# An encoder layer with split weights: high and low activations pass a rounded weight together in one 512-column matmul, and key products on 64 rows

## The chip, the core and the metric

The kernel runs on one core of a Trainium2 chip. Five engines work side by side: TensorE (matmuls; PE in the profile, its weight loads PEld), VectorE (DVE), ScalarE (ACT), GpSimd (POOL) and SyncE (SP, which here only issues transfers). TensorE writes its results into PSUM banks of 128 x 512 float32; VectorE and ScalarE read them there. Transfers run on 16 shared DMA engines. The metric is the device time of one execution, in microseconds, as the median of several runs.

## The reference

One layer of an encoder over 256 tokens of 2048 features, everything in float32:

```python
def reference(x, mem, ...):
    h = layer_norm(x, ln_in_g, ln_in_b)
    for l in range(DEPTH):                      # DEPTH = 1
        mix = hybrid_mixer(h, w_in[l], ...)
        h = layer_norm(ALPHA * h + mix, ln1_g[l], ln1_b[l])
        xa = memory_cross_attention(h, mem, ...)
        h = layer_norm(ALPHA * h + xa, ln2_g[l], ln2_b[l])
        ff = swiglu(h, ffn_wg[l], ffn_wu[l], ffn_wd[l])
        h = layer_norm(ALPHA * h + ff, ln3_g[l], ln3_b[l])
    return h
```

The mixer multiplies h by one wide matrix w_in and feeds two recurrences over time from its columns: a gated linear one (RG-LRU, with a convolution over four steps before it) and a matrix-valued one with 32 heads of 64 (RWKV-7), in which each step rewrites a 64 x 64 state: `S = S*w - (S kk) b^T + v k^T`, output `S r`. Both are gated, added and multiplied by w_out. Then follow attention with 4 heads over 256 memory tokens, and the feed-forward part `(silu(h wg) * (h wu)) wd` with 5632 inner features.

## The kernel before

**Products with streamed weights.** Every large matrix is read once, in halves of 128 x 1024 float32 (512 KB). Matmuls run in a reduced float32 type. To keep precision, each operand is split into two parts: the value rounded to that type (high) and the remainder (low). `split_half` (lines 146 to 156) loads a half into one of four buffers, ScalarE makes the high part `wh` (line 153), VectorE the low part `wl` (line 155), into three buffers each. Of the four products high x high, high x low, low x high and low x low the last is left out.

`wstat` (lines 158 to 169) is used where the result is wanted with features on partitions: a tile of 128 output features by 256 tokens, summed over 16 blocks of 128 input features, eight blocks in each half. The weight block is stationary (loaded into the array), the activations move. For each block line 164 multiplies `wh` by the high activations and line 165 the same `wh` by the low ones, 256 columns each; after eight blocks line 168 multiplies the eight `wl` blocks by the high activations. So a half has 24 matmuls of 256 columns, and a tile uses half a bank. `wtile` (line 174) takes a bank and calls it; its result is a region of PSUM that the consumer reads. It is called for the early and late memory keys (312, 812), all columns of w_in (361, 498, 674, 688, 695, 727), queries (827) and the gate and up products (886, 889). `xstat` (line 179) is the other form, for w_out, the memory values, the attention's output and the down product: there the activations are stationary and 512 columns of the weights move (lines 192, 193, 196). High and low activations are separate tiles of 128 x 256 that `pair_tiles` (line 204) makes.

**The mixer.** For each of four groups of heads (`rwkv_group`), each with four tiles, `tile_stage` (line 425) asks for the tiles k, r and v of w_in and defers the small work on them by a number of weight halves: `key_direction` normalises the key, builds the products' left operand `bk` and copies it on POOL's queue into the padded tile `bz` (lines 458 and 459), in which each head of 64 rows has its own copy with zeros in the other 64 rows; `receptance` fills the other half of the right operand `kr` (465, 466); `products` (line 487) multiplies, for each of two heads and four chunks of 64 steps, 128 padded rows of `bz` by `kr`, in one bank per head, and line 493 masks each bank into `gt`. When a group is complete, `recurrence` solves a triangular system by 31 pairs of small VectorE instructions (lines 532 to 537), sends the result through memory, and after a wait counted in weight halves (`PACE`) `chunk_steps` runs the recurrence over chunks (line 557 on). Between these stand the tiles of the other recurrence (`lru_pair`, line 655, with `recurrent_gates` at 658) and the gates (`gate_group`, line 724).

**What sets the order.** A planner orders each engine's instructions at compile time: it follows priorities (`stream` puts weight loads, splits and the reading of finished banks ahead of all else) and modelled times. At run time each engine keeps that order and waits at its head. Two instructions that touch the same bank are kept apart. In the mixer two accumulator banks serve `wtile`, later four. The pool `mixps` (tag `mix`) has two banks for the small products.

Of the kernel before, what the change touches and what calls it, by code (L numbers as in the profile page):

```python
# [18 lines left out]
P = 128  # L19
T = 256  # L20
# [26 lines left out]
def trunk(ctx, tc, x, memT, vec, rows, consts, lruw, loraw, w_in, w_out, wq, wk, wv, wo, wgu, wd, out,  # L47
# [50 lines left out]
    accs = [None]  # L98
    dram = ctx.enter_context(tc.tile_pool(name="dram", bufs=1, space=bass.MemoryType.DRAM))

    # ---------------------------------------------------------------- constants
# [43 lines left out]
    # ---------------------------------------------------------------- streamed products  # L145
# [11 lines left out]

    def wstat(src, xh, xl, acc):
        for hf in range(2):
            h, l = split_half(src, hf)  # L160
            for kk in range(8):
                k = hf * 8 + kk
                w = h[:, kk * P:(kk + 1) * P]
                nc.tensor.matmul(acc, w, xh[k], start=(k == 0), stop=False)  # L164
                nc.tensor.matmul(acc, w, xl[k], start=False, stop=False)  # L165
            for kk in range(8):
                k = hf * 8 + kk
                mm = nc.tensor.matmul(acc, l[:, kk * P:(kk + 1) * P], xh[k], start=False, stop=(k == 15))  # L168
# [5 lines left out]
    def wtile(src, xh, xl):  # L174
        a = new_acc()[:, 0:T]
        wstat(src, xh, xl, a)
        return a
# [25 lines left out]

    def pair_tiles(pool, n, tag):
        hs = [pool.tile([P, T], F32R, name=f"{tag}h{k}", tag=f"{tag}h{k}") for k in range(n)]
        ls = [pool.tile([P, T], F32R, name=f"{tag}l{k}", tag=f"{tag}l{k}") for k in range(n)]
        return hs, ls

    # ---------------------------------------------------------------- layer norm
# [51 lines left out]
    # ================================================================ input norm  # L261
    h0_d = dram.tile([P, 2, 2048], F32, name="h0_d")
    xTh, xTl = pair_tiles(base, NK, "xT")
    # ================================================================ mixer
# [4 lines left out]
    with ExitStack() as mx:  # L269
# [14 lines left out]
        # ---- first memory keys while the input is normalised  # L284
# [26 lines left out]
        def early_key(k):  # L311
            a = wtile(wk[k], mTh, mTl)
            kr = boot.tile([P, T], F32, name="kr", bufs=2)
            with stream(32):
                nc.scalar.copy(kr, a)
# [21 lines left out]
        # ---- persistent buffers with zeroed parts  # L337
        bz = grp.tile([P, 2, 4, P], F32, name="bkz")
        nc.gpsimd.memset(bz, 0.0)
# [18 lines left out]
        # ---- low-rank inputs  # L358
# [11 lines left out]
        def decay_rates(g, jp, rates):  # L370
            # ---- decay and in-context rate, two tiles
# [53 lines left out]
        def tile_stage(g, j, i, u, fs, av, ev, dt, kr, bkt, sv, yb, gt):  # L425
# [3 lines left out]
            def key_direction():  # L429
                # even chunk: [r'|kk'], [k''|b']; odd chunk: [kk'|r'], [b'|k'']  # L430
# [592 lines left out]
```

## Time and profile before

| | |
|---|---|
| three runs, median | 2201.14 us |
| lowest and highest run | 2199.56 and 2203.24 us |
| the profiled execution, span | 2197.7 us |
| mean granted TensorE clock | 0.990 |
| weight data read and other reads, whole run | 375 MB at a mean of 175 GB/s with the writes |

The profiled execution's own time is its span, from the first instruction to the last; no other time is given for it. By stage, from the view of windows (busy microseconds in each):

| stage | from and to, us | PE | DVE | ACT |
|---|---|---|---|---|
| keys, input norm, mixer | 0 to 970 | 931 | 720 | 512 |
| w_out, attention | 970 to 1440 | 456 | 293 | 212 |
| gate and up products | 1440 to 1940 | 500 | 253 | 216 |
| down product | 1940 to 2183 | 240 | 117 | 92 |
| last norm, output | 2183 to 2198 | 0 | 11 | 2 |

How to read the profile's lines: a group's line has the line of the kernel, the engine, the operation, what it writes and reads (by the program's names), shapes and count; then the total busy time in microseconds, the mean of one in nanoseconds, and the idle time of the engine just before such instructions, with what ended most of it. A timeline line has start, duration, engine, line, operation and, in brackets, the idle time before. A TensorE matmul's duration covers its way through the array and overlaps with that of its neighbours. A float32 matmul of the mixer's small products (not of the reduced type) leaves two records. A window's line has its length, busy time and count for PE, PEld, DVE, ACT and POOL, then the granted TensorE clock, the share of DMA engines at work and GB/s.

### The profile page before, as it was taken

To read this page: it belongs to the slowest core of one execution; us is meant where nothing else is said; L and a number is where in the kernel's file an instruction comes from. 1 tells how busy PE (TensorE), PEld (TensorE's weight loads), DVE (VectorE), ACT (ScalarE), POOL (GpSimd) and SP (SyncE) were. 2 spreads that over 40 slices of the span, in tenths; PEclk is the share of its full clock that TensorE was granted. 3 is DMA by queue.
4 is the path that set the end of the run, shared out by engine and by line. 5 is a ranking of instruction groups with operands and counts; after the bars stand their busy time and mean duration, and the time that the engine had idled before them with its cause. 6 is when DMAs were issued, how large, how long until landed. Compare 5 with 4: busy or idle time off the path is not lost.

```text
span 2197.7 us, 38943 instructions
## 1 busy us (share of the span) xinstructions
PE 2127.7 (97%) x15952; PEld 2004.9 (91%) x15952; DVE 1394.3 (63%) x2121; ACT 1031.9 (47%) x1442; POOL 102.8 (5%) x137
## 2 busy tenths in 40 slices
PE   7999999999999999989999999999999999999996
PEld 7999899999999999877988998799999999988885
DVE  7778676967695769567854555674444444444445
ACT  6646444554455445554544444354444444443332
POOL 1200010011001100200100000000000000000001
PEclk9999999999999999999999999999999999999998
DMA  8555445554555465467565545566555555555563
GB/s 301 186 166 172 140 130 171 177 153 139 176 168 154 139 180 183 123 223 247 183 206 194 165 140 165 190 198 200 184 182 183 184 184 183 182 188 194 192 193 124
DMA packets 149939, 392.41 MB, mean 179 GB/s; under 512 B 39296, under 2 KB 58624, under 8 KB 149248
## 3 DMA queue, kind: packets, MB, share of 16 engines
q1 hardware_dynamic: 137776, 368.81, 52.6%
q10 hardware_dynamic: 9296, 13.24, 2.4%
q0 software_dynamic: 2688, 7.87, 1.2%
q8 instruction: 125, 2.05, 0.4%
q14 instruction: 54, 0.44, 0.1%
HBM read 375.05 MB, written 10.62 MB: 175 GB/s over the span
## 4 chain that ended last, share of the span: by engine, by line
PE 82%; DVE 8%; DMA 6%; issue 2%; ACT 2%; ACTq 0%; POOL 0%; SPq 0%; DVEq 0%; POOLq 0%
PE acc L168 17%; PE acc L165 17%; PE acc L164 17%; PE acc L193 7%; PE acc L192 7%; PE acc L196 7%; DVE wl L155 3%; DVE pd L534 2%; DMA gb<-in_rows_dram 1%; PE mix L491 1%; DVE xi L537 1%; PE rec L590 1%; PE rec L615 1%; DMA bkz<-bk 1%; PE rec L597 1%
## 5 line engine op out<-in xcount | busy, mean ns | idle before, releaser
L155 DVE TENSOR_TENSOR wl<-raw,wh 128x1024 fp32r<-128x1024 f32 x656 | 800.7, 1222 | 581.9 <-ACT wh L153 539.7
L153 ACT CAST wh<-raw 128x1024 fp32r<-128x1024 f32 x656 | 687.4, 1049 | 869.6 <-PE acc L165 535.2
L164 PE MATMUL acc<-xTh,wh 128*128 128x256 f32 x3520 | 881.1, 287 | 1.5 <-DVE ge L694 0.8
L165 PE MATMUL acc<-xTl,wh 128*128 128x256 f32 x3520 | 875.7, 285 | 1.2 <-DVE xTl L248 0.8
L165 PEld LDWEIGHTS acc<-xTl,wh 128*128 128x128 f32 x3520 | 677.9, 193 | 4.5 <-DVE xTl L248 1.2
L164 PEld LDWEIGHTS acc<-xTh,wh 128*128 128x128 f32 x3520 | 677.3, 193 | 4.8 <-DVE ge L694 1.4
L168 PE MATMUL acc<-xTh,wl 128*128 128x256 f32 x3520 | 503.8, 284 | 1.3 <-DVE wl L155 1.3
L168 PEld LDWEIGHTS acc<-xTh,wl 128*128 128x128 f32 x3520 | 457.0, 192 | 3.6 <-DVE wl L155 2.1
L193 PE MATMUL acc<-wh,fl 128*128 128x512 f32 x352 | 136.9, 389 | 0.0
L192 PE MATMUL acc<-wh,fh 128*128 128x512 f32 x352 | 136.9, 389 | 0.0
L196 PE MATMUL acc<-wl,fh 128*128 128x512 f32 x352 | 108.4, 389 | 0.0
L196 PEld LDWEIGHTS acc<-wl,fh 128*128 128x128 f32 x352 | 66.1, 188 | 13.8
L193 PEld LDWEIGHTS acc<-wh,fl 128*128 128x128 f32 x352 | 66.1, 188 | 13.7
L192 PEld LDWEIGHTS acc<-wh,fh 128*128 128x128 f32 x352 | 66.0, 188 | 13.6
L534 DVE TENSOR_TENSOR pd<-xi,al 128x2 f32<-128x2 f32 (+30 forms) x124 | 63.0, 508 | 2.4
L603 POOL TENSOR_SCALAR dms<-ct,dm 128x128 f32<-128x128 f32 x48 | 39.1, 826 | 496.4 <-DVE smat L609 423.3
L890 DVE TENSOR_TENSOR fsg<-fsg,acc 128x256 f32<-128x256 f32 x44 | 18.5, 420 | 61.9 <-PE acc L168 61.4
L192 PE MATMUL acc<-wh,Ah 128*128 128x512 f32 x128 | 50.6, 395 | 0.0
L193 PE MATMUL acc<-wh,Al 128*128 128x512 f32 x128 | 50.6, 395 | 0.0
L192 PE MATMUL acc<-wh,oTh 128*128 128x512 f32 x128 | 49.9, 390 | 0.0
L193 PE MATMUL acc<-wh,oTl 128*128 128x512 f32 x128 | 49.8, 389 | 0.0
L193 PE MATMUL acc<-wh,Bl 128*128 128x512 f32 x128 | 49.8, 389 | 0.0
(267 smaller groups left out, 2265.4 us busy)
## 6 DMA issues: line engine op xcount, KB each, us to landing
raw<-in_w_in_dram SPq DMA_DIRECT2D x232, 512.0 KB, 4.0
raw<-in_wgu_dram SPq DMA_DIRECT2D x176, 512.0 KB, 4.7
raw<-in_wd_dram SPq DMA_DIRECT2D x88, 512.0 KB, 4.6
raw<-in_wk_dram SPq DMA_DIRECT2D x32, 512.0 KB, 4.8
raw<-in_w_out_dram SPq DMA_DIRECT2D x32, 512.0 KB, 5.3
raw<-in_wv_dram SPq DMA_DIRECT2D x32, 512.0 KB, 4.8
raw<-in_wq_dram SPq DMA_DIRECT2D x32, 512.0 KB, 4.1
raw<-in_wo_dram SPq DMA_DIRECT2D x32, 512.0 KB, 4.4
```

The lines of the kernel that those rows point to most:

```text
L153: nc.scalar.copy(h, raw)
L155: nc.vector.tensor_tensor(l, raw, h.bitcast(F32), ALU.subtract)
L164: nc.tensor.matmul(acc, w, xh[k], start=(k == 0), stop=False)
L165: nc.tensor.matmul(acc, w, xl[k], start=False, stop=False)
L168: mm = nc.tensor.matmul(acc, l[:, kk * P:(kk + 1) * P], xh[k], start=False, stop=(k == 15))
L192: nc.tensor.matmul(pt[tt], xh[k][:, ts], w, start=(first and kk == 0), stop=False)
L193: nc.tensor.matmul(pt[tt], xl[k][:, ts], w, start=False, stop=False)
L196: nc.tensor.matmul(pt[tt], xh[k][:, ts], l[:, kk * 512:(kk + 1) * 512], start=False, stop=(last and kk == 1))
L491: nc.tensor.matmul(ps[:, c * P:(c + 1) * P], bz[:, hh, c, :], kr[:, c, :], start=True, stop=True)
L534: nc.vector.tensor_tensor(pd[:, 0:nj, 0:t + 1], xi[:, 0:nj, 0:t + 1], al[:, 0:t + 1, t].rearrange("p (o s) -> p o s", o=1) .broadcast_to([ ...
L537: nc.vector.tensor_reduce(xi[:, 0:nj, t], pd[:, 0:nj, 0:t + 1], AX.X, ALU.add, negate=True)
L603: nc.gpsimd.tensor_scalar(dms[:, j * P:(j + 1) * P], smask, dm[:, j, c:c + 1], None, ALU.mult)
```

## The change

High and low activations of a block become the two halves of one tile of 128 x 512 (`pair`), and lines 164 and 165 become one matmul of 512 columns whose result fills a whole bank: the left half sums high x high, the right half high x low. Line 168 adds low x high to the left half as before. When a tile's sum is complete, `wtile` has ScalarE copy the right half to SBUF and VectorE add the left half to it, in a pool `joins` with two buffers for each; its result is now an SBUF tile, and all consumers read that. Where the old code copied a finished bank to SBUF at once (early keys, line 315; the convolution's input, line 677), the add writes there and the copy is gone. In the key products the padded tile `bz`, its zeroing and its two copies per tile are gone: each product takes the 64 rows of its head from `bk` and `kr` directly, and the two heads alternate, chunk by chunk, between two banks that are taken together.

```diff
+    joins = [None]
+    joins[0] = ctx.enter_context(tc.tile_pool(name="joins", bufs=2))
...
+    both, keep = {}, []
+
     def wstat(src, xh, xl, acc):
         for hf in range(2):
             h, l = split_half(src, hf)
             for kk in range(8):
                 k = hf * 8 + kk
                 w = h[:, kk * P:(kk + 1) * P]
-                nc.tensor.matmul(acc, w, xh[k], start=(k == 0), stop=False)
-                nc.tensor.matmul(acc, w, xl[k], start=False, stop=False)
+                nc.tensor.matmul(acc, w, both[id(xh[k])], start=(k == 0), stop=False)
             for kk in range(8):
                 k = hf * 8 + kk
-                mm = nc.tensor.matmul(acc, l[:, kk * P:(kk + 1) * P], xh[k], start=False, stop=(k == 15))
+                mm = nc.tensor.matmul(acc[:, 0:T], l[:, kk * P:(kk + 1) * P], xh[k], start=False,
+                                      stop=(k == 15))
             passed(mm.ins)
...
-    def wtile(src, xh, xl):
-        a = new_acc()[:, 0:T]
+    def wtile(src, xh, xl, out=None):
+        a = new_acc()
         wstat(src, xh, xl, a)
-        return a
+        with stream(32):
+            t = joins[0].tile([P, T], F32, name="jl")
+            nc.scalar.copy(t, a[:, T:2 * T])
+            if out is None:
+                out = joins[0].tile([P, T], F32, name="js")
+            nc.vector.tensor_tensor(out, a[:, 0:T], t, ALU.add)
+        return out
...
+    def pair(pool, name, tag):
+        t = pool.tile([P, 2 * T], F32R, name=name, tag=tag)
+        h = t[:, 0:T]
+        both[id(h)] = t
+        keep.append(h)
+        return h, t[:, T:2 * T]
+
     def pair_tiles(pool, n, tag):
-        hs = [pool.tile([P, T], F32R, name=f"{tag}h{k}", tag=f"{tag}h{k}") for k in range(n)]
-        ls = [pool.tile([P, T], F32R, name=f"{tag}l{k}", tag=f"{tag}l{k}") for k in range(n)]
-        return hs, ls
+        ps = [pair(pool, f"{tag}{k}", f"{tag}{k}") for k in range(n)]
+        return [h for h, _ in ps], [l for _, l in ps]
...
         def early_key(k):
-            a = wtile(wk[k], mTh, mTl)
             kr = boot.tile([P, T], F32, name="kr", bufs=2)
-            with stream(32):
-                nc.scalar.copy(kr, a)
+            wtile(wk[k], mTh, mTl, out=kr)
             nc.sync.dma_start(k_d[k], kr)
...
-        bz = grp.tile([P, 2, 4, P], F32, name="bkz")
-        nc.gpsimd.memset(bz, 0.0)
...
-                nc.gpsimd.dma_start(bz[0:64, 0], bk[0:64])
-                nc.gpsimd.dma_start(bz[64:128, 1], bk[64:128])
                 q["bk"], q["kf"] = bk, kf
...
             def products():
+                pt = [mps(), mps()]
+                for c in range(4):
+                    for hh in range(2):
+                        rows = slice(64 * hh, 64 * hh + 64)
+                        nc.tensor.matmul(pt[hh][:, c * P:(c + 1) * P], q["bk"][rows, c, :], kr[rows, c, :],
+                                         start=True, stop=True)
                 for hh in range(2):
-                    ps = mps()
-                    for c in range(4):
-                        nc.tensor.matmul(ps[:, c * P:(c + 1) * P], bz[:, hh, c, :], kr[:, c, :],
-                                         start=True, stop=True)
+                    ps = pt[hh]
...
-                ua = wtile(w_in[52 + 3 * i], xTh, xTl)
-                ur = wk1.tile([P, T], F32, name="ur", tag="ge", bufs=2)
-                with stream(32):
-                    evac[0] = nc.scalar.copy(ur, ua)
-                ua = ur
+                ua = wk1.tile([P, T], F32, name="ur", tag="ge", bufs=2)
+                wtile(w_in[52 + 3 * i], xTh, xTl, out=ua)
                 uc = wk1.tile([P, T], F32, name="uc", bufs=2)
                 with stream(32):
-                    nc.scalar.activation(uc, ua, AF.Identity, scale=col("conv3", i), bias=col("conv_b", i))
+                    evac[0] = nc.scalar.activation(uc, ua, AF.Identity, scale=col("conv3", i),
+                                                   bias=col("conv_b", i))
```

The rest of the diff follows from this: queries, attention weights and outputs are made with `pair`, tags of reused tiles lose their h and l, and comments are gone.

More of the change, by code (lines that the diff above doesn't have):

```diff
@@ L766, in trunk @@
         for k in range(NT - 4):
-            yr = ap1.tile([P, T], F32, name="yr", tag=f"Bh{k}")
+            yr = ap1.tile([P, T], F32, name="yr", tag=f"B{k}")
             nc.gpsimd.dma_start(yr, y_d[k])
@@ L823, in trunk @@
             b0 = 4 * (hd % 2)
-            qh = [ap1.tile([P, T], F32R, name="qh", tag=f"Bh{b0 + k}") for k in range(4)]
-            ql = [ap1.tile([P, T], F32R, name="ql", tag=f"Bl{b0 + k}") for k in range(4)]
+            qs = [pair(ap1, "q", f"B{b0 + k}") for k in range(4)]
+            qh, ql = [h for h, _ in qs], [l for _, l in qs]
             for k in range(4):
@@ L828, in trunk @@
                 split_to(a, qh[k], ql[k])
-            pTh = [ap1.tile([P, T], F32R, name="pTh", tag=f"Bh{8 + b0 // 2 + m}") for m in range(2)]
-            pTl = [ap1.tile([P, T], F32R, name="pTl", tag=f"Bl{8 + b0 // 2 + m}") for m in range(2)]
+            pp = [pair(ap1, "pT", f"B{8 + b0 // 2 + m}") for m in range(2)]
+            pTh, pTl = [h for h, _ in pp], [l for _, l in pp]
             pn = []
@@ L842, in trunk @@
                 nc.vector.tensor_reduce(mxx, s, AX.X, ALU.max)
-                pe = ap1.tile([P, NMEM], F32, name="pe", tag=f"Bh{12 + b0 // 2 + tt}")
+                pe = ap1.tile([P, NMEM], F32, name="pe", tag=f"B{12 + b0 // 2 + tt}")
                 nc.vector.tensor_scalar(pe, s, mxx, None, ALU.subtract)
@@ L864, in trunk @@
                     nc.tensor.matmul(o, vl[m][:, cs], pTh[m], start=False, stop=(m == 1))
-                oTh[kk] = ap1.tile([P, T], F32R, name="oTh", tag=f"Ah{kk}")
-                oTl[kk] = ap1.tile([P, T], F32R, name="oTl", tag=f"Al{kk}")
+                oTh[kk], oTl[kk] = pair(ap1, "oT", f"A{kk}")
                 split_to(o, oTh[kk], oTl[kk])
```

## The prediction

> **What bounds the kernel now.** I read the page first (busy time, then the chain that ended last), then the DMA issues, to count the work that is edited, then TensorE's timeline for the price of one matmul, and last the windows and waits of the stage where other engines are loaded. The page:
>
> ```profile
> span 2197.7 us, 38943 instructions
> PE 2127.7 (97%) x15952; PEld 2004.9 (91%) x15952; DVE 1394.3 (63%) x2121; ACT 1031.9 (47%) x1442; POOL 102.8 (5%) x137
> PE 82%; DVE 8%; DMA 6%; issue 2%; ACT 2%; ACTq 0%; POOL 0%; SPq 0%; DVEq 0%; POOLq 0%
> PE acc L168 17%; PE acc L165 17%; PE acc L164 17%; PE acc L193 7%; PE acc L192 7%; PE acc L196 7%; DVE wl L155 3%; DVE pd L534 2%; DMA gb<-in_rows_dram 1%; PE mix L491 1%; DVE xi L537 1%; PE rec L590 1%; PE rec L615 1%; DMA bkz<-bk 1%; PE rec L597 1%
> ```
>
> TensorE stands 97% busy, and 82% of the chain is its own. The three lines that the change edits (164, 165, 168) are 17% each: half of the span. Matmuls overlap, so what counts isn't the duration of one but the distance between two starts. Two stretches where nothing waits, one with 256 moving columns (the gate and up products) and one with 512 (the down products, where activations are stationary):
>
> ```profile
> 1900.62 0.28 PE L164 MATMUL acc<-xTh,wh 128*128 128x256 f32 x1
> ...
> 1902.42 0.28 PE L165 MATMUL acc<-xTl,wh 128*128 128x256 f32 x1
> 1902.54 1.12 PE L168 MATMUL acc<-xTh,wl 128*128 128x256 f32 x8
> 1903.50 0.28 PE L164 MATMUL acc<-xTh,wh 128*128 128x256 f32 x1
> ```
>
> ```profile
> 2000.81 0.39 PE L192 MATMUL acc<-wh,fh 128*128 128x512 f32 x1
> ...
> 2001.72 0.62 PE L196 MATMUL acc<-wl,fh 128*128 128x512 f32 x2
> 2002.17 0.39 PE L192 MATMUL acc<-wh,fh 128*128 128x512 f32 x1
> ```
>
> The first stretch is one half of a weight tile: 24 matmuls in 1903.50 - 1900.62 = 2.88 us, 0.1200 us each. The second is 6 matmuls in 2002.17 - 2000.81 = 1.36 us, 0.2267 us each. Doubling the columns adds 0.1067 us, so each matmul carries 0.0133 us that doesn't grow with its columns.
>
> **The pairs that become one.** Which products go through the edited function shows in the transfers of weight halves:
>
> ```profile
> raw<-in_w_in_dram SPq DMA_DIRECT2D x232, 512.0 KB, 4.0
> raw<-in_wgu_dram SPq DMA_DIRECT2D x176, 512.0 KB, 4.7
> raw<-in_wk_dram SPq DMA_DIRECT2D x32, 512.0 KB, 4.8
> raw<-in_wq_dram SPq DMA_DIRECT2D x32, 512.0 KB, 4.1
> ```
>
> That is 472 halves (236 tiles) with 8 pairs each: 3776 pairs. A pair costs 0.2400 us now and 0.2267 us as one 512-column matmul, whose shape, type and weight load are those of line 192. Saved: 3776 x 0.0133 = 50.3 us. Of it 1856 pairs (24.7 us) belong to the 116 tiles of w_in, in the mixer, and 1920 (25.6 us) to keys, queries and the feed-forward part. The eight matmuls of line 168 per half stay at 0.1200. The bounds are 0 (should the fixed part not go away) and 50.3; I take 50.3, since the row of line 192 is the very form.
>
> The Trainium skill ("TensorE: Matmul & The Clock Gate", section Back-to-back issue gap) puts the gap at columns / 2.4 + 2.5 ns. By that a pair would save only 2.5 ns and the term would be an estimated 9.4 us. The two stretches above disagree, with 13.3 ns; the measurement decides for the sum, and the page's figure returns as a rival.
>
> **The join that each tile gains.** For each of 236 tiles ScalarE copies the upper half of the bank (0.370 us by line 677) and VectorE adds the lower half (0.417 us by line 202), before the old consumer starts:
>
> ```profile
> L155 DVE TENSOR_TENSOR wl<-raw,wh 128x1024 fp32r<-128x1024 f32 x656 | 800.7, 1222 | 581.9 <-ACT wh L153 539.7 <-PE acc L168 20.4 <-ACT rhsz L593 8.7
> L153 ACT CAST wh<-raw 128x1024 fp32r<-128x1024 f32 x656 | 687.4, 1049 | 869.6 <-PE acc L165 535.2 <-PE acc L193 257.3 <-DVE wl L155 10.1
> L677 ACT COPY ur<-acc 128x256 f32<-128x256 f32 x16 | 5.9, 370 | 0.0
> L202 DVE TENSOR_TENSOR ql<-acc,qh 128x256 fp32r<-128x256 f32 x16 | 6.7, 417 | 0.0
> ```
>
> That is 87 us of ScalarE (less 21 copies of lines 315 and 677 that go, 8 us) and 98 us of VectorE. Whether it costs time depends on the stage:
>
> ```profile
> 0.00:970.00 970.00, 931.04 (x7986) 900.59 (x7987) 719.89 (x1278) 511.67 (x784) 86.92 (x125) 0.99 0.55 170
> 600.00:650.00 50.00, 50.00 (x399) 49.26 (x398) 46.32 (x97) 26.64 (x41) 0.00 (x0) 1.00 0.58 176
> 1500.00:1900.00 400.00, 400.00 (x3335) 400.00 (x3335) 193.61 (x209) 169.13 (x209) 0.00 (x0) 1.00 0.57 183
> ```
>
> (Length, then busy PE, PEld, DVE, ACT, POOL.) In the feed-forward part 70 tiles of 5.76 us add 29 us to DVE's 194 of 400 and 26 to ACT's 169: covered by the 400 us of TensorE, at no cost. A half then comes every 8 x 0.2267 + 8 x 0.1200 = 2.77 us in place of 2.88; the 2.72 us that a half takes in the down products is already faster, so the loads follow.
>
> In the mixer DVE goes from 720 to 768 of 970 us: not bound on the average. But from 600 to 650, where a long chain of small VectorE instructions (the triangular solve, lines 534 and 537) runs between the weight splits, 9 joins of 0.417 take DVE from 46.3 to 50.1 of 50: full. There the solve ends later. Its 62 instructions in the last group, and the waits of TensorE behind it and behind the recurrent gates:
>
> ```profile
> 825.54 0.16 DVE L534 TENSOR_TENSOR pd<-xi,al 128x2 f32<-128x2 f32 x1
> ...
> 871.24 0.68 DVE L537 TENSOR_REDUCE xi<-pd 128x16 f32<-128x512 f32 x1
> ```
>
> ```profile
> 246.40 0.80 PE L558 MATMUL rec<-x1z,gt 128*32 128x32 f32 x11 [2.30 <-DVE x1z L552]
> 882.68 1.20 PE L558 MATMUL rec<-x1z,gt 128*32 128x32 f32 x32 [3.33 <-DVE x1z L552]
> 672.30 1.70 PE L661 MATMUL lrups<-uc,lrw 128*128 128x256 f32 x4 [2.19 <-ACT ii L665]
> ```
>
> The solve takes 46.4 us; 8 joins in it make it 3.3 us longer, and TensorE, faster by 0.107 us a half over about 20 halves, comes 2.1 us sooner. In the first and the last group TensorE already waits for its result (2.30 and 3.33 us), so up to 5.4 us more there, 10.8 in all; nothing, if the compiled order puts the solve's consumers behind more weight matmuls, since the order follows from modelled times. For the wait of line 661 (three of this size) one copy and one add more stand in the queues: up to 2.4 us. Bounds 0 and 13.2; no row shows the new order, so I take a little over the middle: 8 us. What is queued behind a waiting join is the next weight cast or split; three buffers of each cover that by two halves, 5.5 us. In attention the four heads' scores get their queries 0.79 us later, 0 to 3.2 us; the next head's query products stand beside them, so I take 1.
>
> **The key products.** Removed are two DMAs on POOL's queue per tile (32 in all), one memset, and TensorE's wait for them; the eight products per tile go to 64 rows, alternating between two banks:
>
> ```profile
> 109.23 1.95 PE L491 MATMUL mix<-kkr,bkz 128*128 128x128 f32 x16
> 110.93 0.36 PE L164 MATMUL acc<-xTh,wh 128*128 128x256 f32 x1
> ...
> 331.71 0.28 DVE L466 TENSOR_TENSOR kkr<-zr,dtg 128x128 f32<-128x128 f32 x1
> 333.11 2.05 PE L491 MATMUL mix<-kkr,bkz 128*128 128x128 f32 x16 [2.28 <-DMA bkz<-bk]
> ```
>
> ```profile
> L491 PE MATMUL mix<-kkr,bkz 128*128 128x128 f32 x256 | 32.1, 277 | 5.1 <-DMA bkz<-bk 5.0
> L493 DVE TENSOR_TENSOR gt<-mix,ct 128x512 f32<-128x512 f32 x32 | 20.9, 683 | 10.8 <-PE mix L491 10.8
> ```
>
> The wait is worth 0 to 5.0 us. In the wait shown, the other operand (line 466) ends at 331.99, so 1.1 of the 2.28 us goes and VectorE is late next: I take 3 of 5. A tile's 16 records take 110.93 - 109.23 = 1.70 us. If the two row halves run at the same time, 0.85 us goes, 13.6 us for 16 tiles; if not, nothing. Against it stands the change of array shape:
>
> ```profile
> 252.83 0.28 PE L165 MATMUL acc<-xTl,wh 128*128 128x256 f32 x1
> 253.04 2.11 PE L567 MATMUL rec<-ymat,zz 128*32 128x32 f32 x64
> ```
>
> 0.21 us before a 32-column form in place of 0.12: 0.09 us, twice in 16 tiles, 2.9 us. And both banks are now full together, with two buffers in that pool: whoever needs one straight afterwards waits for line 493, up to 0.68 us for each of 16 tiles, 10.9 us. Ends: -13.6 and +13.8. No trace here has a 64-row form, so I take the half-way case of the first term with little of the last: -3 us. The Trainium skill ("TensorEngine Tiling (Array Packing)", section Key Properties) says that changing the tiling mode drains TensorE, which speaks against this part; the 0.09 us above agrees in kind.
>
> **The sum.** -50.3 + 8 + 1 - 3 - 3 = -47.3 us. The profiled execution has a span of 2197.7 us; the median of the runs is 2201.14, 3.4 us (0.16%) above, and what lies around the span is unedited. So 2197.7 - 47.3 = 2150.4 for the span and 2153.8, rounded 2154, for the median.
>
> **The rivals.** (A) The mixer gives its whole gain back: its times are set by chains over VectorE, ScalarE and small transfers that don't get faster, and only the 25.6 us of the other parts stay: 2175.5. For it speaks DVE at 46 of 50; against it that PE is busy 931 of the mixer's 970 us, so only 39 us are waits. (B) The compiled order absorbs the joins, and the key products run two at a time (-13.6, less 2.9 for the change of shape and some 3 for the shared banks, so -8): -50.3 - 5 - 8 = -63, 2138. (C) The fixed part of a matmul isn't saved, because a 512-column matmul with activations moving takes two 256-column ones less 2.5 ns: -9.4 us, and with 8 + 1 - 3 - 3 = +3 about 2195. Against it stand the rows of line 192. (D) Slower: the join holds the bank. The mixer has two accumulators, so a bank must be back 5.5 us after its last matmul; a join behind a cast and a split takes 1.05 + 0.37 + 1.22 + 0.42 = 3.1 us, and it waits in order behind the solve. If TensorE stood 0.5 us per mixer tile for a bank or for a late weight split, 116 tiles would cost 58 us on top: 2212; it decides from 47.3 / 116 = 0.41 us a tile. Against it: the 2.4 us left, and two halves of splits ahead.
>
> **How the numbers follow.** Forecast 63%, A 16%, B 12%, C 3%, D 6%. The range, 2136 to 2180, takes in A and B and the unknown terms; C, D and the tails are left out. Within 0.2% (4.4 us, about what a measurement of this kernel can tell from no change) I put 2%, the edge of C and D; slower 6%; faster 92%.
>
> **What would show it.** Right: lines 164 and 165 become one group of 3776 with 512 columns and starts 0.227 us apart; a half takes 2.77 us in the feed-forward part, which shortens by about 19 us; DVE's busy time grows by some 98 us and ACT's by some 79; no wait on bkz is left. The waits of lines 558 and 661 show what the mixer returns. Wrong: starts of 512 columns 0.238 us apart (C), or TensorE waiting for VectorE's joins or splits by over 60 us in the first 970 (D).

## The result and the profile after

Four runs of the changed kernel took 2165.18 to 2166.9 us, median 2165.51; four of the kernel before 2199.56 to 2203.24, median 2201.45. The ratio is 0.9839, with a 95% interval of 0.9825 to 0.9853: 36 us faster. The forecast was 47 us, in a range that holds the result; so the sign and the size are as forecast, 11 us short. What follows is about those 11 us. Most of them turn out to lie in one term, the pairs; the joins cost about what was forecast, but by another way.

The page of the changed kernel, the same four lines as before:

```profile
span 2163.6 us, 31791 instructions
PE 2085.8 (96%) x12176; PEld 1789.3 (83%) x12176; DVE 1476.9 (68%) x2357; ACT 1092.3 (50%) x1656; POOL 80.6 (4%) x104
PE 82%; DVE 10%; DMA 4%; ACT 3%; issue 2%; POOL 0%; SPq 0%; ACTq 0%; DVEq 0%; POOLq 0%
PE acc L168 34%; PE acc L171 17%; PE acc L206 7%; PE acc L202 7%; PE acc L203 7%; DVE wl L157 4%; DMA gb<-in_rows_dram 2%; ACT wh L155 1%; DVE pd L547 1%; DVE xi L550 1%; PE rec L603 1%; PE rec L610 1%; PE rec L628 1%; PE mix L502 1%; PE rec L662 1%
```

TensorE has 3776 matmuls fewer and still carries 82% of the chain. VectorE's busy time rose by 82.6 us and ScalarE's by 60.4, less than the 98 and 79 of the forecast, because instructions overlap more; their durations added up grow by 101.2 and 82.9 us. On the chain VectorE went from 8% to 10%. The groups of the edited lines (busy us, mean ns, idle before, by line and shape):

```profile
L168 PE MATMUL acc<-xT,wh 128*128 128x512 f32 x3520 | 917.1, 399 | 5.7 <-DVE js L186 4.0 <-DVE ur L186 1.0 <-DVE xT L264 0.3
L171 PE MATMUL acc<-xT,wl 128*128 128x256 f32 x3520 | 503.0, 284 | 0.0
L183 ACT COPY jl<-acc 128x256 f32<-128x256 f32 x236 | 86.6, 367 | 22.0 <-PE acc L171 20.1 <-DVE hres L275 1.0
L186 DVE TENSOR_TENSOR js<-acc,jl 128x256 f32<-128x256 f32 x215 | 90.0, 419 | 3.4 <-ACT jl L183 3.1
```

The joins cost what the prediction's rows said: 0.367 us a copy, 0.419 us an add.

**Where the time went, by stage.** The first and last start of groups on the accumulator banks show where a stage begins and ends: the products of w_out (operand `A`) end the mixer, those of the down product (`f`, before `fh`) end the gate and up products. Before:

```profile
L192 PE MATMUL acc<-wh,fh x352: 389/389/396, 1940.9 to 2179.4; 128*128 128x512 f32 x176
...
L192 PE MATMUL acc<-wh,Ah x128: 389/389/628, 962.4 to 1057.9; 128*128 128x512 f32 x128
```

After:

```profile
L202 PE MATMUL acc<-wh,f x352: 389/389/396, 1907.3 to 2145.8; 128*128 128x512 f32 x176
...
L202 PE MATMUL acc<-wh,A x128: 389/389/628, 946.5 to 1042.5; 128*128 128x512 f32 x128
```

The end of w_out moved by 1057.9 - 1042.5 = 15.4 us, where the prediction's terms gave about 23.8 (24.7 of pairs in the mixer and 1.1 for the five early keys that stand ahead of it, 8 lost at the joins, 3 and 3 won at the key products). The start of the down product moved by 33.6. From one to the other it took 883.0 us and takes 864.8: 18.2 us, where the terms gave 23.5 (24.5 of pairs less 1). From there on nothing changed, as nothing was edited.

**Inside a half.** TensorE's timeline in the gate and up products, where it never stands still:

```profile
1700.62 2.00 PE L168 MATMUL acc<-xT,wh 128*128 128x512 f32 x8
1702.46 1.11 PE L171 MATMUL acc<-xT,wl 128*128 128x256 f32 x8
1703.41 1.32 PE L168 MATMUL acc<-xT,wh 128*128 128x512 f32 x5
```

A half takes 1703.41 - 1700.62 = 2.79 us (2.793 on the mean of the stage), not the 2.773 of the prediction. The eight wide matmuls take 1.84 us where 8 x 0.2267 is 1.81; the narrow ones 0.95 where 8 x 0.12 is 0.96. The single starts in the trace say where it lies: the first five wide matmuls after a run of narrow ones start 233, 236, 228, 233 and 231 ns apart, the following ones 227; the first narrow matmul's successor comes after 113 ns, the others after 119 to 120. It was so, place by place, in all 167 halves of that stage whose 16 matmuls are in the trace.

**The waits.** TensorE's waits (us in total, times, longest), before:

```profile
PE acc L164 <- ACT mh L307: 7.9, 2, 7.1
PE lrups L661 <- ACT ii L665: 6.5, 3, 2.5
...
PE rec L558 <- DVE x1z L552: 5.6, 2, 3.3
...
PE mix L491 <- DMA bkz<-bk: 5.0, 4, 2.3
```

And after:

```profile
PE lrups L674 <- ACT ii L678: 12.2, 4, 3.6
PE acc L168 <- DVE m L325: 9.0, 2, 6.6
...
PE mix L447 <- DVE gt L506: 3.4, 7, 0.5
...
PE rec L571 <- DVE x1z L565: 0.2, 1, 0.2
```

The wait for the padded copy is gone, as forecast. The wait for the triangular solve (`x1z`), which the prediction expected to grow, is gone too, though the solve itself grew. Its 62 instructions in the last group:

```profile
808.53 0.16 DVE L547 TENSOR_TENSOR pd<-xi,al 128x2 f32<-128x2 f32 x1
...
866.82 0.68 DVE L550 TENSOR_REDUCE xi<-pd 128x16 f32<-128x512 f32 x1
```

They take 59.0 us in place of 46.4: 12.6 us more, where the prediction had 3.3. In place of the solve's wait the wait of the recurrent gates for their single bank (`lrups`, given back by ScalarE's `ii`) nearly doubled, and line 447 (the key's norm) now waits for a `mixps` bank that line 506 still reads.

**The clock behind a wait.** A wait of TensorE costs more than its length. Behind the solve's wait of 3.33 us in the kernel before, and behind the gates' wait of 3.29 us that ends at 226.4 us in the changed kernel, TensorE works at a granted clock of 0.50 (third number from the end):

```profile
884.40:887.80 3.40, 3.40 (x40) 3.17 (x39) 2.40 (x6) 0.63 (x2) 0.00 (x0) 0.50 0.70 276
```

```profile
226.40:232.30 5.90, 5.87 (x18) 5.03 (x19) 5.74 (x10) 2.71 (x5) 0.00 (x0) 0.50 0.68 230
```

In the first of these stretches the 256-column matmuls start 0.21 us apart in place of 0.12. In the changed kernel's trace each wait of 3.0 us or more after the first 20 us goes with such a stretch, of 3.4 or 6.8 us; of the shorter waits some do. Up to the end of w_out they add up to 23.9 us before and 30.7 after. TensorE loses about half of such a stretch, so up to there 12.0 us before and 15.4 after: 3.4 us more. The prediction priced a wait by its length and had this at nothing. The amount differs from one execution to the next: the kernel `e_swap_ffn` below has the same mixer, and its profile shows 41.0 us and an end of w_out at 1048.4 in place of 1042.5.

VectorE was as full as forecast, 49.33 us of 50 against 50.1; TensorE, busy in all 50 of them before, now in 47.51. In the gate and up products it is busy 400 of 400, with the joins beside it:

```profile
600.00:650.00 50.00, 47.51 (x265) 41.42 (x264) 49.33 (x92) 28.00 (x48) 0.00 (x0) 1.00 0.49 164
1500.00:1900.00 400.00, 400.00 (x2292) 351.98 (x2291) 226.98 (x287) 191.34 (x287) 0.00 (x0) 1.00 0.56 189
```

### The profile page after: what moved, and what is told of

It reads as the page before. It is cut to its first block, busy times and chain, and to the rows that moved or that the text cites. A ratio compares the mean times of both kernels' runs of the same rounds, so it can differ in the third digit from the quotient of the medians.

```text
span 2163.6 us, 31791 instructions
## 1 busy us (share of the span) xinstructions
PE 2085.8 (96%) x12176; PEld 1789.3 (83%) x12176; DVE 1476.9 (68%) x2357; ACT 1092.3 (50%) x1656; POOL 80.6 (4%) x104
## 4 chain that ended last, share of the span: by engine, by line
PE 82%; DVE 10%; DMA 4%; ACT 3%; issue 2%; POOL 0%; SPq 0%; ACTq 0%; DVEq 0%; POOLq 0%
PE acc L168 34%; PE acc L171 17%; PE acc L206 7%; PE acc L202 7%; PE acc L203 7%; DVE wl L157 4%; DMA gb<-in_rows_dram 2%; ACT wh L155 1%; DVE pd L547 1%; DVE xi L550 1%; PE rec L603 1%; PE rec L610 1%; PE rec L628 1%; PE mix L502 1%; PE rec L662 1%
## 5 line engine op out<-in xcount | busy, mean ns | idle before, releaser
L168 PE MATMUL acc<-xT,wh 128*128 128x512 f32 x3520 | 917.1, 399 | 5.7 <-DVE js L186 4.0
L168 PEld LDWEIGHTS acc<-xT,wh 128*128 128x128 f32 x3520 | 636.2, 190 | 123.8 <-DVE js L186 4.7
L171 PEld LDWEIGHTS acc<-xT,wl 128*128 128x128 f32 x3520 | 484.0, 191 | 36.0
L171 PE MATMUL acc<-xT,wl 128*128 128x256 f32 x3520 | 503.0, 284 | 0.0
L203 PE MATMUL acc<-wh,f 128*128 128x512 f32 x352 | 136.9, 389 | 0.0
L202 PE MATMUL acc<-wh,f 128*128 128x512 f32 x352 | 136.9, 389 | 0.0
L206 PE MATMUL acc<-wl,f 128*128 128x512 f32 x352 | 108.4, 389 | 0.0
L202 PEld LDWEIGHTS acc<-wh,f 128*128 128x128 f32 x352 | 66.1, 188 | 13.7
L203 PEld LDWEIGHTS acc<-wh,f 128*128 128x128 f32 x352 | 66.0, 188 | 13.7
L203 PE MATMUL acc<-wh,A 128*128 128x512 f32 x128 | 50.5, 396 | 0.5 <-DVE A L212 0.5
L202 PE MATMUL acc<-wh,A 128*128 128x512 f32 x128 | 50.3, 394 | 0.3 <-ACT A L211 0.3
L202 PE MATMUL acc<-wh,oT 128*128 128x512 f32 x128 | 50.0, 391 | 0.0
L203 PE MATMUL acc<-wh,oT 128*128 128x512 f32 x128 | 49.8, 389 | 0.0
L203 PE MATMUL acc<-wh,B 128*128 128x512 f32 x128 | 49.8, 389 | 0.0
L202 PE MATMUL acc<-wh,B 128*128 128x512 f32 x128 | 49.8, 389 | 0.0
```

What stands on the lines that cost most here:

```text
L168: nc.tensor.matmul(acc, w, both[id(xh[k])], start=(k == 0), stop=False)
L171: mm = nc.tensor.matmul(acc[:, 0:T], l[:, kk * P:(kk + 1) * P], xh[k], start=False, stop=(k == 15))
L202: nc.tensor.matmul(pt[tt], xh[k][:, ts], w, start=(first and kk == 0), stop=False)
L203: nc.tensor.matmul(pt[tt], xl[k][:, ts], w, start=False, stop=False)
L206: nc.tensor.matmul(pt[tt], xh[k][:, ts], l[:, kk * 512:(kk + 1) * 512], start=False, stop=(last and kk == 1))
```

## The experiments

The theory after these readings (theory 1 in the first expectations): the pairs bring some 41 us, since the way from narrow to wide matmuls costs 20 ns a half; the key products bring some 9 us; the joins cost some 11 us, through VectorE's and ScalarE's time in the mixer. Its rivals put the missing time elsewhere: on the wide matmuls or on the key products, with joins that cost little. Each kernel ran beside the kernel before on the same chip; ratios are to that, with 95% intervals.

**The key products alone**, in the kernel before: no padded tile, no copies, 64 rows, two banks.

```diff
-                nc.gpsimd.dma_start(bz[0:64, 0], bk[0:64])
-                nc.gpsimd.dma_start(bz[64:128, 1], bk[64:128])
...
+                pt = [mps(), mps()]
+                for c in range(4):
+                    for hh in range(2):
+                        rows = slice(64 * hh, 64 * hh + 64)
+                        nc.tensor.matmul(pt[hh][:, c * P:(c + 1) * P], q["bk"][rows, c, :], kr[rows, c, :],
...
```

> The kernel before with only the key products changed: 64 rows, two banks taken together, no padded copy; weight products and banks as before. Theory 1 (my reading of the two traces): the two row halves run together, so the 16 records of a tile take 1.1 in place of 1.7 us (9 to 10 us in all), the wait for the copies goes (up to 5 us), and the normalisation's matmul waits about 0.65 us for a bank in some 7 of 16 tiles (4.6 us back): 2201 - 10 = 2191 us, a ratio of about 0.9955. Rival (the shared banks eat the gain and the new order costs more): 2201 or above.

Measured: 2192.42 us beside 2199.59, ratio 0.996 (0.9945 to 0.9976), a gain of 7 to 9 us (by medians, by the ratio). That is somewhat more than the 6 us of the prediction, but the interval goes from 5 to 12 us. Two of its waits:

```profile
PE lrups L660 <- ACT ii L664: 6.1, 3, 2.4
...
PE mix L433 <- DVE gt L492: 3.6, 9, 0.4
```

The gates' wait is as it was before (6.5 us), so that its growth in the changed kernel isn't owed to the key products. The wait for a bank at the key's norm is theirs.

**Without the join**: line 183 and line 186 left out, consumers read the left half of the bank. It leaves out the products of high weights with low activations from the result; the matmuls themselves stay.

```diff
-            nc.scalar.copy(t, a[:, T:2 * T])
-            if out is None:
-                out = joins[0].tile([P, T], F32, name="js")
-            nc.vector.tensor_tensor(out, a[:, 0:T], t, ALU.add)
-        return out
+        if out is not None:
+            with stream(32):
+                nc.scalar.copy(out, a[:, 0:T])
+            return out
+        return a[:, 0:T]
```

> The changed kernel without the join: consumers read the left half of the bank as before, so the product of the high weights with the low activations is computed and then left out of the result. Theory 1: the joins lengthen the queues of ScalarE and VectorE in the mixer, and TensorE's waits there grew by 12 us for it; without them about 2165.5 - 12 = 2153 us, while a half in the gate and up stage stays at 2.79 us, because the extra 20 ns come with the step from 256 to 512 columns. Rival 2 (the 20 ns come from the joins' reading and writing beside the matmuls): a half falls to 2.77 us, 9 us more off, 2144 us. Rival 3 (the mixer's new waits come from the key products' shared banks and the new order): at most 3 us faster, 2162 to 2166 us.

Measured: 2154.27 us, ratio 0.9787 (0.9763 to 0.981), 11 us below the changed kernel. A half still takes 2.793 us. So the joins cost 11 us, give or take some 6 by the two ratios' intervals, and the 20 ns per half aren't theirs. By the profiled executions 12.0 us of it lie before the end of w_out (1042.5 against 1030.5) and 3.3 between there and the down product; that profile was taken 4 us under its median, so the split is good to a few us. From the end of w_out to the down product it takes 861.5 us, 21.5 less than the kernel before; 1.7 of these come from 3.4 us less at half clock, and 19.8 are left, where 230 halves at 0.087 us give 19.9. The end of w_out and its waits:

```profile
L200 PE MATMUL acc<-wh,A x128: 389/389/628, 936.1 to 1030.5; 128*128 128x512 f32 x128
```

```profile
PE rec L569 <- DVE x1z L563: 4.0, 1, 4.0
PE lrups L672 <- ACT ii L676: 3.6, 3, 2.3
PE mix L445 <- DVE gt L504: 2.5, 8, 0.3
```

Without joins `lrups` costs 3.6 us in place of 12.2, and the solve's wait is back at 4.0, with a solve of 49.8 us in the last group.

**One step in place of two.** In the second half of a tile the low weights go first, so that narrow and wide matmuls change places once per tile and direction:

```diff
+            if hf == 0:
+                high()
+                mm = low()
+            else:
+                low()
+                mm = high()
```

> The changed kernel with the order turned round in every second half: 512 columns first, then 256, then 256, then 512, so a tile has one step from narrow to wide in place of two. Theory 1 (the extra time sits in the first five wide matmuls after narrow ones): a tile in the gate and up stage takes 5.566 in place of 5.586 us, 236 x 0.020 = 4.7 us off, about 2161 us, and the wide matmuls of the second half are 0.2267 us apart, the first ones too where the next tile follows. Rival 2 (it comes from where the activations of the blocks lie, or from the joins): the slow ones stay at the same blocks, 2165 us.

Measured: 2166.43 us, ratio 0.9849 (0.9825 to 0.9874): no gain in the whole, which was a miss. TensorE's timeline, though, does show the shorter tile:

```profile
1699.42 3.82 PE L169 MATMUL acc<-xT,wh 128*128 128x512 f32 x16
1703.07 2.08 PE L176 MATMUL acc<-xT,wl 128*128 128x256 f32 x16
1704.98 3.82 PE L169 MATMUL acc<-xT,wh 128*128 128x512 f32 x16
1708.64 2.08 PE L176 MATMUL acc<-xT,wl 128*128 128x256 f32 x16
1710.55 0.63 PE L169 MATMUL acc<-xT,wh 128*128 128x512 f32 x2
```

A tile takes 5.56 and 5.57 us where two halves were 5.586: one change from narrow to wide costs 19 to 20 ns. The slow starts moved with the change: they stand in the second half's wide matmuls, while the next tile's first wide ones, behind wide ones, start 227 ns apart. So the cause isn't which block a matmul multiplies. What was won is lost in the mixer, where the low parts are now wanted half a period sooner and VectorE has them late:

```profile
PE acc L176 <- DVE wl L157: 14.1, 12, 2.5
...
PE lrups L686 <- ACT ii L690: 2.0, 2, 1.8
```

**The two heads one after the other**, so that a bank is complete, and read, sooner:

```diff
-                for c in range(4):
-                    for hh in range(2):
+                for hh in range(2):
+                    for c in range(4):
```

> The changed kernel with the key products in head order: four chunks of the first head, then four of the second, still 64 rows. Theory 1 (the gain of this part is that two row halves run together): 16 records take about 1.7 us again, 16 x 0.6 = 9.8 us back, less the 4.6 us of waits for a bank that the earlier end of the first bank saves: about 2170 us. Rival 3 (the shared banks are what costs in the mixer): at or below 2163 us.

Measured: 2165.63 us, ratio 0.9842 (0.9818 to 0.9866): the same as the changed kernel; a few us slower was expected. TensorE's timeline of one tile, first in the changed kernel, then here:

```profile
108.92 1.16 PE L502 MATMUL mix<-kkr,bk 64*128 64x128 f32 x16
110.01 0.98 PE L168 MATMUL acc<-xT,wh 128*128 128x512 f32 x3
111.45 0.67 PE L447 MATMUL mix<-sq,ct 128*128 128x256 f32 x2 [0.46 <-DVE gt L506]
```

```profile
108.67 1.71 PE L502 MATMUL mix<-kkr,bk 64*128 64x128 f32 x16
110.31 0.96 PE L168 MATMUL acc<-xT,wh 128*128 128x512 f32 x3
111.22 0.67 PE L447 MATMUL mix<-sq,ct 128*128 128x256 f32 x2
```

Alternating, the 16 records take 110.01 - 108.92 = 1.09 us, in head order 1.64; that is the row halves at work together. And alternating, line 447 stands 0.46 us for a bank, in head order not at all. 0.55 won, 0.46 returned in this tile. The whole times show no gain of the concurrency; only the timelines show it. So the gain of the key products alone may be owed to the copies that are gone as much as to the two heads running together: no run separates the two.

**Half a join.** Two kernels tell which engine's time the 11 us are: one with ScalarE's copy alone, whose result nobody reads, one with VectorE's instruction alone (a copy of the left half, same size). Both leave out the same products as the kernel without the join.

```diff
             nc.scalar.copy(t, a[:, T:2 * T])
-            if out is None:
-                out = joins[0].tile([P, T], F32, name="js")
-            nc.vector.tensor_tensor(out, a[:, 0:T], t, ALU.add)
-        return out
+            if out is not None:
+                nc.scalar.copy(out, a[:, 0:T])
+                return out
+        return a[:, 0:T]
```

> The changed kernel with ScalarE's copy of the right half kept and read by nobody, and VectorE's add left out: consumers read the left half of the bank, so high weights by low activations is missing from the result. No join at all gave 2154 us, the full join 2165.5. Theory 1a (the cost of the join is VectorE's 0.42 us per tile, on the engine that is nearly full beside the triangular solve): near 2154, at most 2157 us. Theory 1b (the cost is ScalarE's copy at the head of its queue, waiting for the bank while weight casts stand behind it): near 2165 us. Theory 1c (it is the length of the chain, two more hops): between, and the same as the run with the add alone.

```diff
-            nc.scalar.copy(t, a[:, T:2 * T])
...
-            nc.vector.tensor_tensor(out, a[:, 0:T], t, ALU.add)
+            nc.vector.tensor_copy(out, a[:, 0:T])
         return out
```

> The changed kernel with a VectorE copy of the left half in place of ScalarE's copy and VectorE's add: the consumers read that copy; high weights by low activations is missing from the result. Theory 1a (VectorE's time is the cost): near 2165 us. Theory 1b (ScalarE's copy): near 2154 us. Theory 1c (the chain): between the two, near the run with the copy alone.

Measured: copy alone 2153.24 us, ratio 0.9786 (0.9761 to 0.981), as without any join (0.9787). VectorE's alone 2159.71, ratio 0.9818 (0.9794 to 0.9842), 5 to 7 us more. The intervals of the ratios overlap, but three of its four runs lie above all eight of the two kernels without VectorE's work, and the fourth above seven of them. The wait for the gates' bank is long where VectorE has the work; copy alone, then VectorE alone:

```profile
PE lrups L674 <- ACT ii L678: 3.3, 3, 2.9
```

```profile
PE lrups L672 <- ACT ii L676: 11.2, 4, 3.8
```

So the wait, though ScalarE's instruction ends it, comes with VectorE's work, and so does the longer solve (57.3 us in the last group with VectorE's instruction alone, 50.1 with the copy alone). None of the sharp cases of the expectation holds as it stands: by the medians half of the cost comes with VectorE's instruction and the other half only with both, but with intervals of some 5 us to either side that share is rough.

**A third bank.** If the price is a bank, a bank should buy it back. The gates' own pool had one, `mixps` two; here all three are one pool:

```diff
-        mp = mx.enter_context(tc.tile_pool(name="mixps", bufs=2, space=PSUM))
+        mp = mx.enter_context(tc.tile_pool(name="mixps", bufs=3, space=PSUM))
...
-        lp = mx.enter_context(tc.tile_pool(name="lrups", bufs=1, space=PSUM))
...
-                ps = lp.tile([P, 512], F32, name="lrups")
+                ps = mps()
```

> The changed kernel with the single bank of the recurrent gates given to the pool of small products, which so has three banks for both. TensorE waits 13 us before the recurrent gates for their one bank (held by ScalarE's reading in a queue that the joins made longer), and 4.6 us before the normalisation's matmul for one of the two banks that the key products fill together. If these waits are for banks (theory 1), both go nearly: about 2165.5 - 13 = 2152 us. If the queues behind them are what is late (rival: the gates' inputs and the mask wait in the same queues), TensorE meets them a step later: 2162 to 2166 us.

Measured: 2152.58 us, ratio 0.9783 (0.9763 to 0.9804), 13 us below the changed kernel. The waits that the expectation counts at 13 and 4.6 us are 12.2 and 3.4 in the view shown above. Neither the gates nor the key's norm wait for a bank now; the solve, with 59.3 us in the last group as long as with two banks, has its wait back:

```profile
PE rec L570 <- DVE x1z L564: 6.6, 2, 3.3
PE acc L168 <- DVE js L186: 5.6, 4, 1.9
...
PE acc L171 <- DVE wl L157: 2.3, 2, 1.4
```

The end of w_out:

```profile
L202 PE MATMUL acc<-wh,A x128: 387/389/628, 933.9 to 1028.3; 128*128 128x512 f32 x128
```

**The shorter tile where TensorE hardly waits**: the order of the one-step kernel for the gate and up products only.

```diff
+            if hf == 0 or not swap[0]:
+                high()
+                mm = low()
+            else:
+                low()
+                mm = high()
```

> The changed kernel with the turned order of the second halves (256 columns first, then 512) in the gate and up products alone; the mixer and attention keep theirs. With the order turned everywhere the steps were fewer but TensorE waited 14 us for low weight parts in the mixer, where VectorE is late. In the gate and up stage nothing waits, so the steps saved should show whole: 88 x 0.020 = 1.8 us off a stage of 488.9 us, about 2163.7 us. If the turned order costs waits there too: 2165.5 or more.

Measured: 2165.97 us, ratio 0.9848 (0.9827 to 0.987). A gate or up tile takes 5.567 us there as in the one-step kernel, but 88 tiles x 19 ns are 1.7 us, and the interval is wider than that: no gain can be told from the whole times. The profiles show 504.3 us in place of 505.2 from the attention's output to the down product, so 0.9 of the 1.7 us; a wait of 0.8 us for a low part, at the stage's start, accounts for the rest.

**What the joins cost when there is a third bank**: both edits, without the join (leaving out the same products) and with `mixps` of three.

```diff
-        with stream(32):
-            t = joins[0].tile([P, T], F32, name="jl")
...
+        return a[:, 0:T]
...
+        mp = mx.enter_context(tc.tile_pool(name="mixps", bufs=3, space=PSUM))
```

> Three shared banks for the small products and the recurrent gates, and no join (consumers read the left half of the bank; high weights by low activations is missing from the result). With one bank for the gates the join cost 11 us. If that cost was TensorE's wait for this bank, which the longer queues hold (theory 1), the join costs little here: three banks gave 2152.6 us with the join, so 2149 to 2152 without. If the join's cost is VectorE's time in general (rival), it shows here too: about 2141 us.

Measured: 2146.35 us, ratio 0.9737 (0.9711 to 0.9763). Against the three-bank kernel that is 6 us by medians and 10 by the ratios. It lies between the two theories. The end of w_out:

```profile
L200 PE MATMUL acc<-wh,A x128: 387/389/628, 933.9 to 1026.0; 128*128 128x512 f32 x128
```

Two readings stand against each other. By the profiles, w_out ends at 1028.3 with joins and 1026.0 without, so with three banks the mixer gives 2.3 us for the joins where it gave 12.0 with the old pools; and from there to the down product 2.7. With half of the stretches at half clock taken off, the ends are 1027.1 (and 1027.9 in `e_swap_ffn`) with joins and 1013.4 without for the old pools, and 1014.7 (and 1013.0 in `e_mix3_swap_ffn`, the last run below) with joins and 1010.6 without for three banks. That reading makes most of the mixer's cost the bank. By the whole times it isn't: without joins the third bank brings 2154.27 - 2146.35 = 8 us (11 by the ratios), nearly as much as the 13 (12) with joins. The waits that it ends there are the 3.6 us of `lrups` and the 2.5 of the key's norm. The ratios' intervals, some 5 us to either side, leave both readings standing, so how much of the joins' cost is the bank isn't shown.

**A third bank for the kernel before**, which tells whether the pool was short all along:

```diff
-        mp = mx.enter_context(tc.tile_pool(name="mixps", bufs=2, space=PSUM))
+        mp = mx.enter_context(tc.tile_pool(name="mixps", bufs=3, space=PSUM))
...
+                ps = mps()
```

> The kernel before with the recurrent gates' bank given to the pool of small products (three banks), all else as before. There TensorE waits 6.5 us for that bank, half of what it waits in the changed kernel. If three banks take these waits away in both kernels: about 2200 - 7 = 2193 us, and the change is then worth about 41 us in place of 36. If the bank is only late because of the join: 2200 us.

Measured: 2201.41 us over ten runs beside 2202.09, ratio 0.9993 (0.9978 to 1.0008): nothing. The 6.5 us at `lrups` are gone, and others of the same size are there:

```profile
PE acc L164 <- DVE ge L693: 7.4, 5, 2.7
...
PE rec L557 <- DVE x1z L551: 6.0, 2, 4.6
```

So the third bank is worth something only beside the change; it isn't a repair that the old kernel could have had as well. But "beside the change" isn't "beside the joins": without them it still brought 8 us. The key products, which now fill two banks together, and TensorE's faster pace are the other candidates; a third bank beside the key products alone was not tried.

**Three banks and the shorter gate and up tiles**, the best version at hand:

```diff
+        mp = mx.enter_context(tc.tile_pool(name="mixps", bufs=3, space=PSUM))
...
+            if hf == 0 or not swap[0]:
```

> The changed kernel with three shared banks in the mixer and, in the gate and up products alone, the order turned in every second half. Three banks gave 2152.6 us; the turned order takes 0.8 to 1.8 us off the gate and up stage: about 2151 us.

Measured: 2151.28 us, ratio 0.9765 (0.9746 to 0.9784), 51 us below the kernel before. It can't be told from three banks alone (0.9783, 0.9763 to 0.9804).

## Why the prediction came out as it did

**The pairs: the mechanism right, the term too large.** The failed step is "A pair costs 0.2400 us now and 0.2267 us as one 512-column matmul, whose shape, type and weight load are those of line 192". In a run of wide matmuls that holds: they settle at 227 ns. So the mechanism is right, and the size isn't. But line 192 stood only among wide matmuls, and here eight wide and eight narrow ones alternate; each return to wide costs 20 ns. A half falls from 2.880 to 2.793 us, 0.087 in place of 0.107, and 472 halves, at the price of the gate and up products, give 40.9 us in place of 50.3. The steps cost 9.4 us of the forecast, and the one-step order shows that they are steps: half as many, half the cost per tile.

The rival (C), in which a pair saves only 2.5 ns, fell: in steady runs the starts stand 120.0 ns apart at 256 columns and 226.7 at 512, so a pair would save 13.3 ns, and with the steps it saves 10.8. The Trainium skill ("TensorE: Matmul & The Clock Gate", Back-to-back issue gap) gives its 2.5 ns for a matmul by itself; in the streams of this trace it is 13.3 ns.

**The joins: a fair size, by the wrong way.** Forecast were 8 us in the mixer and 1 in attention, measured 11 in all; that the sizes agree is in part luck. The solve does get longer, by 12.6 us in the last group in place of 3.3. The failed step is that TensorE pays for it, "up to 5.4 us more there, 10.8 in all": in the changed kernel TensorE waits 0.2 us for the solve, not 5.6 and more. In the last group it waits 3.6 us for the gates' bank first, in the newly compiled order, and asks for the solve's result 12 us after the solve's end, when it is there. The prediction had allowed for such an order ("nothing, if the compiled order puts the solve's consumers behind more weight matmuls") and took a middle. It had the gates' wait as its smaller item, up to 2.4 us; it grew by 5.7. VectorE's time was the root, as the prediction had it: it is full from 600 to 650, the solve and the gates' wait grow where it has the work, and the copy on ScalarE alone costs nothing. That the feed-forward part hides its joins (400 of 400 busy) was right.

**The key products: right in kind, perhaps too small.** Forecast were 3 us for the wait and 3 for the products, measured 7 to 9 together in the kernel before, with an interval that holds the 6. The trace shows what the half-way case was made of: the row halves do run together where the order alternates, 0.6 us less per tile, in ten of sixteen tiles. In the six others, five of them directly behind the transposes of line 494, the compiled order took one head's chunks ahead of the other's and a tile took 1.83 us or more. In the run of this part alone it was thirteen of sixteen, so that in the changed kernel it may be worth some 2 us less (three tiles at 0.74). And the price for the two banks being full together was there, 3.4 us at line 447. The Trainium skill ("TensorEngine Tiling (Array Packing)", Key Properties) says that tiles of the array work independently; the trace agrees, with starts of the two row halves 6 to 7 ns apart. Its other rule, that a change of mode drains the array, shows in no total here: one start of each tile comes after 207 ns in place of 105, and a gain was left.

**The sum.** -40.9 for the pairs, +11 for the joins, -7 to -9 for the key products: -37 to -39, beside -36 measured, inside the intervals. What the half clock costs isn't a term of its own here; it is part of what was measured. The wide matmul was not run by itself; its 40.9 us come from the length of a half, not from a run without the rest.

**The rivals.** The mixer did not give everything back (A): its end came 15.4 us earlier. The slow case (D), a stand of over 0.41 us per tile at the accumulators, shows in the waits with 4.0 us for `js` and 2.6 for late low parts in all. Of B, the two heads do run together, though not in every tile, but the joins are not absorbed.

**What stays open.** How the joins' 11 us split: VectorE's instruction alone costs 5 to 7, ScalarE's alone nothing, both 11; with three banks 6 to 10 by the whole times, 5 by the profiles. With that, whether the bank or VectorE's time is what they cost, and what the third bank pays for without them. Why a matmul stream needs five matmuls to settle after a change of width was not tried.

## What to carry to other kernels

The price of a matmul form read from a stretch of equal matmuls is that of a steady run; where forms alternate, count the changes as well, and put equal forms side by side if the next operand is there in time. When an edit loads a busy engine further, follow its delay to the buffers with one copy: the wait shows there under another engine's name, ahead of the chain that one was watching. When one more buffer brings as much as a part of the edit costs, that doesn't yet show that it pays for this part: try it without the part, and without the edit. Here it brought 13 us with the joins, 8 without them, and nothing in the kernel before. And count a wait of TensorE of some 2 us or more above its length, as the clock may be halved for the next 3.4 us.

## What the runs showed of the hardware

Coming from 256-column matmuls, the first five of 512 columns start 228 to 236 ns apart, and only then 227; the second narrow one after wide ones comes after 113 ns in place of 120; the net cost is 19 to 20 ns for each return to wide. Float32 matmuls on the two row halves of the array, into two banks, start 6 to 7 ns apart when their order alternates, and 16 records take 1.09 us, where they took 1.70 on 128 padded rows; in head order on 64 rows they take 1.64. Behind a wait of TensorE the granted clock can be 0.50 for 3.4 or 6.8 us: it was so at each wait of 3.0 us or more after the first 20 us of the changed kernel, and in the kernel before at one of 1.9 us.
